# Keys and first values of six gated-DeltaNet heads as seven block products instead of eight

## The chip, the cores and the metric

The kernel runs on one core of one Trainium2 chip. The metric is the device time of one execution in microseconds (us), the median over runs; lower is better. TensorE (PE in the profile) multiplies, VectorE (DVE), ScalarE (ACT) and GpSimd (POOL) do elementwise work, and SyncE (SP) issues nearly all DMAs.

## The reference

Two residual layers over 1024 tokens of width 1024: a gated DeltaNet layer (GDN), then an mLSTM layer, then a final RMSNorm. The change is in the GDN layer, which has 8 heads of 128 key and 256 value columns:

```
p = h @ w_in                                    # h: (1024 tokens, 1024), w_in: (1024, 6160)
qkv, z, a, bt = split(p)
qkv = silu(causal_dwconv(qkv, conv_w))          # 4 taps along the tokens
q = l2norm(q) * 128**-0.5 ;  k = l2norm(k)      # per head
o = gated_delta_chunked(q, k, v, g, beta)       # per head, chunks of tokens, state carried
o = rmsnorm(o, norm_w) * silu(z)
y = o @ w_out
```

Within a head and a chunk, `gated_delta_chunked` forms k k^T with decays, solves a unit lower triangular system, and then walks through the chunks one after the other with a 128 x 256 state.

## The kernel before, in words

**Number format.** Each fp32 operand of a large product is split into two fp32r parts, `hi` (a rounded copy, made on ACT, L261) and `lo` (the rest, made on POOL, or on DVE where an engine is given, L262). A product of two operands is three matmuls: hi*hi, hi*lo, lo*hi. The activations h stand in SBUF transposed, as tiles of 128 features x 512 tokens (two halves of the tokens), split the same way.

**Projection.** A head's 768 columns of `w_in` (128 key, 128 query, 256 value, 256 gate columns z) are computed as three sources of work of two 128-column blocks each: keys with first values (`gkv`), queries with second values (`gqv`), and both gate blocks (`gzp`). The features and the tokens are cut in two, so two column blocks against two token halves are four results, each a sum over two feature halves: eight block products of 4 x 3 = 12 matmuls of 128x512. `Columns` makes the eight products; with `sums=True` it uses A11, S1 = A21 + A22, A12 and A22 of the activations, with the second half's weights as differences. `Pair` makes the same four results from seven products (Strassen's scheme in Winograd's form) with sums S1 to S4 of activation blocks, which stand ready from head 2 on, and with sums of weight blocks, made on DVE; its partial results are then added up on DVE out of PSUM. Before the change, heads 2 to 7 use `Columns(sums=True)` for `gkv` and `Pair` for `gqv` and `gzp`: 32 + 28 + 28 = 88 steps, where a step is three matmuls of 128x512.

**Order of the work.** TensorE's order is written out by hand: the generators of all heads' products run one after the other, and after the n-th step of a head the small generators that stand in `plan` for that step issue their own work. The tables `KEYS`, `QUERIES`, `SOLVE`, `MERGE`, `TOKENS`, `SCAN` (steps after the head's first one; the last entry holds for heads 2 to 7) and `PACE` place them. A number past the head's length falls into the next head. The other engines' orders are set by a scheduler when the program is built. Each engine runs its own list in order; a waiting instruction holds up everything behind it there.

**What a head does besides**, by its functions: `conv_silu` takes a finished result, multiplies and adds the four taps (ACT L291, DVE L298) and applies SiLU (ACT L301). `gdn_keys` transposes the keys (`tpk`), squares them on ACT (`sqrk`), forms `kd`, loads a row of decays (`growb`, DMA), forms the mask `at` = exp(growb + mask - g) with DVE L877 and ACT L880, forms `kk` = k k^T on PE and `nt` on DVE L893, and sends `nt` through DRAM into `nd` (L899, L902). `gdn_solve` runs 31 pairs of small DVE operations on `nd` (`pr`, `xt`, L939 and L941) and sends the result through DRAM into `td`. `gdn_merge` completes the inverse: a DVE product and two transposes give `t`, then four rounds of small matmuls `xp`, `yp`, `xl`, `yl` with copies in between, five steps of the plan, each 4 steps behind the last. `gdn_scan` walks over the 8 chunks: `ks` (PE), `rr` (DVE), `y` (PE), `w` (ACT), `sn` (PE), new state `S` (DVE), `o` (PE), and a transpose `go` for the output gate. `gdn_tokens` transposes the values (`gvp`). The scan, the merge and the tokens of head h run among the products of head h+1.

**Buffers.** PSUM has eight banks, by tags: p 2, b 1, x 1, c 2 (scan), d 2 (all of `tpk`, `kk`, `kq`, `gvp`, `go` and the four merge rounds share these two). In SBUF the tag `rowb` has one buffer of 128x512: `growb` of both halves (and the decay rows of the queries) pass through it, and also the running sum u2 of `gqv`. A buffer is given to the next tile once the last reader of the present one is done, also where that reader comes later in the program.

Of the kernel before, what the change touches and what calls it, by code (L numbers as in the profile page):

```python
# [9 lines left out]
F32 = mybir.dt.float32  # L10
# [3 lines left out]
ALU = mybir.AluOpType  # L14
# [3 lines left out]
P = 128  # L18
# [5 lines left out]
DK = 128  # L24
# [34 lines left out]
TOKENS = ((37, 37, 81, 85), (71, 74, 97, 103), (64, 68, 107, 110))  # L59
# [9 lines left out]
def hybrid_kernel(ctx, tc, x_in, norm_w, final_norm_w, gdn_w_in, gdn_conv_w, gdn_a_log, gdn_dt_bias, gdn_norm_w,  # L69
# [18 lines left out]
    def pwork(name, tag="b"):  # L88
        return pw.tile([P, 512], F32, tag=tag, bufs=banks[tag], name=name)
# [166 lines left out]
    def split(raw, name, tiles=None, e=None, scale=None):  # L256

        shape = list(raw.shape)
        hi, lo = tiles or (wp.tile(shape, F32R, tag=f"ws_{n}", bufs=3, name=f"{name}_{n}") for n in ("hi", "lo"))
        if scale is None:  # L260
            A.copy(hi, raw)  # L261
            (e or G).tensor_tensor(lo, raw, hi.bitcast(F32), ALU.subtract)  # L262
# [209 lines left out]
    def product(ps, block, parts, first=True):  # L472

        hi, lo = parts
        for k, (bhi, blo) in enumerate(blocks[block]):
            if k:
                yield
            for i, (w_, h_) in enumerate(((hi, bhi), (hi, blo), (lo, bhi))):
                mm(ps, w_[:, k, :], h_, start=first and k == 0 and i == 0, stop=k == 3 and i == 2,  # L479
                   skip_group_check=True)  # L480
# [12 lines left out]
    class Columns:  # L493
# [32 lines left out]

        def products(self):
            for e, tags in enumerate(("pp", "bx")):
                ps = [pwork(f"{self.name}_ps{e}{half}", tags[half]) for half in range(2)]
                top = operand()  # L530
                yield from product(ps[0], "A11", top)
                yield
                yield from product(ps[1], "S1" if self.sums else "A21", top)
                yield
                for half in range(2):
                    if half == 0 or self.sums:
                        bottom = operand()
                    yield from product(ps[half], ("A12", "A22")[half], bottom, False)
                    self.sink(e, half, ps[half])
                    yield  # L540

    class Pair:
# [31 lines left out]
        def products(self):  # L574
# [39 lines left out]
            sink(0, 1, c21)  # L614
            yield


    ready, sources = [], []

# [9 lines left out]
    def operand():  # L629
        ahead(LOOK + 1)  # L630
        return ready.pop(0)
# [160 lines left out]
    def gdn_columns(h, st):  # L792

        st["vt"], st["v"] = {}, []

        def dst(e):
            def of(half):
                t = st["vt"][e, half] = hp.tile([P, TH], F32, tag="acc", bufs=3, name=f"gvT{h}_{e}_{half}")
                return t

            return of

        vs = [conv_silu(gcw, 32, 2 * H + 2 * h + e, dst(e), f"gv{h}_{e}") for e in range(ET)]
        v0 = 2 * QK + h * DV
        sinks_of = lambda *sinks: lambda e, half, src: sinks[e](half, src)
        if h == 0:
            return [Columns(gdn_w_in, v0, v0 + P, f"gv{h}", sinks_of(*vs), small=True)]
        k = qk_sink("k", gcw, 32, h, st, "g")
        q = qk_sink("q", gcw, 32, h, st, "g")
        first = Columns(gdn_w_in, QK + h * DK, v0, f"gkv{h}", sinks_of(k, vs[0]), sums=h > 1)  # L810
        if h == 1:
            return [first, Columns(gdn_w_in, h * DK, v0 + P, f"gvq{h}", sinks_of(q, vs[1]))]
# [254 lines left out]
    with tc.manual_schedule(engines={mybir.EngineType.PE}):  # L1067
# [555 lines left out]
```

## Time and profile before

| | |
|---|---|
| median of 3 runs | 1989.7 us (1989.58 to 1993.05) |
| profiled execution: time / span | 1988.66 us / 1986.9 us |
| PE busy | 1900.5 us, 96% of the span |
| DVE busy | 1293.0 us, 65% |
| ACT busy | 1010.6 us, 51% |
| POOL busy | 699.9 us, 35% |
| mean granted TensorE clock | 0.984 |

How to read it: the GDN heads 2 to 7 run from 234.8 to 800.95 us of the span. A busy share of PE of 96% doesn't say that matmuls run at their rate, since the durations of neighbouring matmuls overlap; the distance between their starts does.

### The profile page before, as it was taken

The numbers are of one execution on the slowest core, as the hardware profiler recorded it, in microseconds if no ns is written. First come the engines' busy times: TensorE is split into PE (matmuls) and PEld (weight loads), VectorE is DVE, ScalarE is ACT, GpSimd is POOL, SyncE is SP. The second block draws the span as 40 slices with busy tenths as digits, with TensorE's granted clock in tenths as the row PEclk, the third lists the DMA queues.
The fourth block names the chain that finished last, engine by engine and source line by source line (L and its number), as shares of the span: only waits on it lengthen the run. The fifth ranks groups of instructions, "written<-read, shape, count | busy, mean of one in ns | idle before, by whom it ended". The sixth has DMA issues, their size and how long they took to land.

```text
span 1986.9 us, 28860 instructions
## 1 busy us (share of the span) xinstructions
PE 1900.5 (96%) x9768; PEld 1561.3 (79%) x9768; DVE 1293.0 (65%) x2911; ACT 1010.6 (51%) x2325; POOL 699.9 (35%) x621
## 2 busy tenths in 40 slices
PE   5989999999999999999999899999999999999987
PEld 3777787878787878787878778888888888878876
DVE  7688586858595858548555966666766666673313
ACT  5435454646465555546435555545454555564423
POOL 4243333333333333101021434343333333354553
PEclk9999999999999999999999999999999999999988
DMA  4211122222222222646321122212122222246332
GB/s 139 87 38 51 54 70 70 62 76 58 77 62 67 70 67 77 193 124 219 122 75 55 59 80 65 74 59 75 54 85 64 75 67 65 79 137 204 104 117 75
DMA packets 138620, 171.24 MB, mean 86 GB/s; under 512 B 30860, under 2 KB 68584, under 8 KB 138472
## 3 DMA queue, kind: packets, MB, share of 16 engines
q1 hardware_dynamic: 138472, 169.40, 27.4%
q8 instruction: 77, 1.26, 0.3%
q14 instruction: 71, 0.58, 0.1%
HBM read 142.87 MB, written 26.48 MB: 85 GB/s over the span
## 4 chain that ended last, share of the span: by engine, by line
PE 73%; DVE 14%; DMA 5%; ACT 4%; issue 3%; POOL 1%; SPq 1%; DVEq 0%; ACTq 0%; POOLq 0%
PE lout L678 8%; PE gout L678 7%; PE mv_ps L479 6%; PE gkv_ps L479 6%; PE mkq_ps L479 6%; PE mz_ps L479 6%; PE mog_ps L479 6%; PE gqv_ps L479 5%; PE gzp_ps L479 3%; DMA growb<-g_dram 1%; PE mo L1452 1%; PE mv_ps L1209 1%; DVE gvT L298 1%; PE y L1020 1%; PE out L383 1%
## 5 line engine op out<-in xcount | busy, mean ns | idle before, releaser
L393 POOL TENSOR_TENSOR g_r<-g_r,mhalf 128x1 f32<-128x1 f32 x64 | 41.0, 640 | 220.5 <-DVE g_r L392 203.0
L267 DVE SCALAR_TENSOR_TENSOR gw_lo<-gw_raw,rest,gw_hi 128x256 fp32r<-128x256 f32 x128 | 61.0, 513 | 66.0 <-ACT gw_hi L266 63.4
L262 POOL TENSOR_TENSOR lw_lo<-lw_raw,lw_hi 128x512 fp32r<-128x512 f32 x56 | 72.8, 1302 | 74.9 <-ACT lw_hi L261 71.2
L678 PE MATMUL lout<-lgp_hh,lw_hi 128*128 128x512 f32 x224 | 89.4, 399 | 4.3 <-DVE y L1411 3.2
L262 POOL TENSOR_TENSOR mog_lo<-mog_raw,mog_hi 128x512 fp32r<-128x512 f32 x39 | 50.5, 1294 | 114.5 <-ACT mog_hi L261 114.5
L262 POOL TENSOR_TENSOR mz_lo<-mz_raw,mz_hi 128x512 fp32r<-128x512 f32 x39 | 53.8, 1381 | 98.3 <-ACT mz_hi L261 98.3
L678 PE MATMUL lout<-lgp_hl,lw_hi 128*128 128x512 f32 x224 | 88.4, 395 | 0.0
L678 PE MATMUL lout<-lgp_hh,lw_lo 128*128 128x512 f32 x224 | 87.3, 394 | 0.0
L266 ACT ACTIVATE gw_hi<-gw_raw,rest 128x256 fp32r<-128x256 f32 x128 | 58.1, 502 | 55.2 <-PE gout L678 38.9
L262 POOL TENSOR_TENSOR mv_lo<-mv_raw,mv_hi 128x512 fp32r<-128x512 f32 x38 | 52.0, 1369 | 83.9 <-ACT mv_hi L261 48.0
L479 PE MATMUL gkv_ps<-hh,gkv_hi 128*128 128x512 f32 x176 | 81.3, 462 | 0.0
L262 POOL TENSOR_TENSOR gkv_lo<-gkv_raw,gkv_hi 128x512 fp32r<-128x512 f32 x40 | 52.7, 1317 | 78.2 <-ACT gkv_hi L261 65.9
L262 POOL TENSOR_TENSOR gzp_lo<-gzp_raw,gzp_hi 128x512 fp32r<-128x512 f32 x38 | 49.7, 1309 | 68.0 <-ACT gzp_hi L261 57.0
L261 ACT CAST lw_hi<-lw_raw 128x512 fp32r<-128x512 f32 x56 | 34.8, 621 | 75.2 <-PE lout L678 56.5
L262 POOL TENSOR_TENSOR mkq_lo<-mkq_raw,mkq_hi 128x512 fp32r<-128x512 f32 x35 | 47.1, 1347 | 71.5 <-ACT mkq_hi L261 60.7
L479 PE MATMUL gkv_ps<-hh,gkv_lo 128*128 128x512 f32 x176 | 70.4, 400 | 0.0
L479 PE MATMUL gkv_ps<-hl,gkv_hi 128*128 128x512 f32 x176 | 70.4, 400 | 0.0
L393 POOL TENSOR_TENSOR m_r<-m_r,mhalf 128x1 f32<-128x1 f32 x64 | 44.9, 702 | 71.9 <-DVE m_r L392 70.9
L678 PE MATMUL gout<-glp_hh,gw_hi 128*128 128x512 f32 x160 | 66.7, 417 | 0.0
L678 PE MATMUL gout<-glp_hl,gw_hi 128*128 128x512 f32 x160 | 62.6, 391 | 0.0
L678 PE MATMUL gout<-glp_hh,gw_lo 128*128 128x512 f32 x160 | 62.6, 391 | 0.0
L262 POOL TENSOR_TENSOR gqv_lo<-gqv_raw,gqv_hi 128x512 fp32r<-128x512 f32 x30 | 38.6, 1288 | 65.1 <-PE sn L1027 25.2
(761 smaller groups left out, 6735.6 us busy)
## 6 DMA issues: line engine op xcount, KB each, us to landing
gw_raw<-in_gdn_w_out_dram SPq DMA_DIRECT2D x64, 256.0 KB, 2.6
lw_raw<-in_mlstm_w_out_dram SPq DMA_DIRECT2D x56, 256.0 KB, 2.7
gzp_raw<-in_gdn_w_in_dram SPq DMA_DIRECT2D x32, 256.0 KB, 3.2
growb<-g_dram SPq DMA_DIRECT2D x32, 256.0 KB, 3.1
gg_dram<-gv_h SPq DMA_DIRECT2D x64, 128.0 KB, 1.9
gl<-gg_dram SPq DMA_DIRECT2D x32, 256.0 KB, 3.4
mog_raw<-in_mlstm_w_in_dram SPq DMA_DIRECT2D x32, 256.0 KB, 3.2
mz_raw<-in_mlstm_w_in_dram SPq DMA_DIRECT2D x32, 256.0 KB, 3.0
```

Of the source, the lines that this page charges most:

```text
L261: A.copy(hi, raw)
L262: (e or G).tensor_tensor(lo, raw, hi.bitcast(F32), ALU.subtract)
L266: A.activation(hi[:, k], raw[:, k], AF.Copy, scale=c)
L267: V.scalar_tensor_tensor(lo[:, k], raw[:, k], c, hi.bitcast(F32)[:, k], ALU.mult, ALU.subtract)
L298: V.scalar_tensor_tensor(d_[:, d:], ps[:, :TH - d], col(3 - d), d_[:, d:], ALU.mult, ALU.add)
L383: mm(ps, a[:, e, ds], b[:, e, hs], start=m == 0, stop=m == 3 * ET - 1)
L393: G.tensor_tensor(r, r, mhalf[:, :1], ALU.pow)
L479: mm(ps, w_[:, k, :], h_, start=first and k == 0 and i == 0, stop=k == 3 and i == 2, skip_group_check=True)
L678: mm(pss[2 * j + i], a[:, e, i * P:(i + 1) * P], b, start=h == heads[0] and e == 0 and m == 0, stop=h == heads[-1] and e == ET - 1 and m == 2)
L1020: mm(yp[:, :DV], st["tt"][half][:, cc, :], rr, start=True, stop=True)
L1209: mm(ps[c], h_[k][half][:, c * P:(c + 1) * P], w_[:, k % 2, :], start=k == 0 and i == 0, stop=k == KT - 1 and i == 2)
L1452: mm(op[:, :DV + 2], q[:, s_], S, start=True, stop=False)
```

## The change

The key and first value blocks of heads 2 to 7 become a subclass of `Pair`, `LeftPair`, with another order of the seven products: both token halves of the keys come first (after steps 12 and 20), both halves of the values last (after step 28). Its u2 takes the `rowb` buffer, and the u2 of `gqv` goes to another one. A head is 84 steps instead of 88, and the tables are moved. Core of the diff:

```diff
-KEYS = ((4, 9, 11, 14), (28, 31, 32, 35), (22, 25, 26, 29))
-QUERIES = ((17, 20, 22, 30), (68, 71, 76, 76), (82, 82, 86, 91))
-SOLVE = (27, 44, 32)
-MERGE = ((78, 82), (86, 93), (86, 100))
+KEYS = ((4, 9, 11, 14), (28, 31, 32, 35), (22, 25, 26, 28))
+QUERIES = ((17, 20, 22, 30), (62, 71, 76, 76), (74, 78, 80, 84))
+SOLVE = (27, 44, 38)
+MERGE = ((78, 82), (86, 93), (90, 100))
...
-SCAN = (91, 113, 102)
-PACE = ((3, 3, 8), (4, 3, 10), (4, 3, 11))
+SCAN = (91, 113, 103)
+PACE = ((3, 3, 8), (4, 3, 10), (4, 3, 9))
...
+    class LeftPair(Pair):
+        def operands(self):
...
+            yield part(1, b11, G)
+            V.tensor_tensor(b12, b12, b22, ALU.subtract)
+            V.tensor_tensor(b11, b11, b12, ALU.subtract)
+            yield part(6, b11, e6)
+            yield part(2, b21, G)
+            yield part(7, b12, G)
+            V.tensor_tensor(b21, b21, b11, ALU.subtract)
+            yield part(4, b21, G)
+            V.tensor_tensor(b11, b22, b11, ALU.subtract)
+            yield part(5, b11, e5)
+            yield part(3, b22, G)
+        def products(self):
...
+            yield from product(p1, "A11", operand())
+            A.copy(u2, p1)
...
+            yield from product(p6, "S2", operand())
+            V.tensor_tensor(u2, u2, p6, ALU.add)
...
+            yield from product(p1, "A12", operand(), False)
+            sink(0, 0, p1)
...
+            yield from product(p7, "S3", operand())
+            V.tensor_tensor(u3, u2, p7, ALU.add)
...
+            yield from product(p7, "A22", operand(), False)
+            V.tensor_tensor(p7, u2, p7, ALU.add)
+            sink(0, 1, p7)
...
+            yield from product(p5, "S1", operand())
+            V.tensor_tensor(u3, u3, p5, ALU.add)
...
+            yield from product(p5, "S4", operand(), False)
+            V.tensor_tensor(p5, u2, p5, ALU.add)
+            sink(1, 0, p5)
+            sink(1, 1, u3)
...
-        first = Columns(gdn_w_in, QK + h * DK, v0, f"gkv{h}", sinks_of(k, vs[0]), sums=h > 1)
...
-        return [first, Pair(gdn_w_in, h * DK, v0 + P, f"gqv{h}", sinks_of(q, vs[1]), u2=(hp, "rowb", 1), in_psum=(True, False),
-                            bank="b")]
+        return [LeftPair(gdn_w_in, QK + h * DK, v0, f"gkv{h}", sinks_of(k, vs[0]), u2=(hp, "rowb", 1), bank="b"),
+                Pair(gdn_w_in, h * DK, v0 + P, f"gqv{h}", sinks_of(q, vs[1]), in_psum=(True, False), bank="b")]
...
-            base += (64, 96)[h] if h < 2 else 88
+            base += (64, 96)[h] if h < 2 else 84
```

What the built programs hold: matmul instructions on PE fall by 72 and POOL's instructions by 6, DVE's rise by 54 and ACT's by 22; the number of DMAs stays. Head 5 serves for the places that the prediction speaks of. In the changed program the lines from L612 on stand 53 lines lower: L877, L880, L893, L939, L991 are L930, L933, L946, L992, L1044 there. Names carry the head, the half and a running number, `gkv5_u2` being the running sum of head 5's first pair.

DVE, where head 5's masks `at` are formed. Before:

```order
L877 TENSOR_TENSOR at5_0_5639<-growb05_0_5637,cmask_128 128x512
L877 TENSOR_TENSOR at5_1_5714<-growb05_1_5712,cmask_128 128x512
L991 COPY tt4_1_5466<-yl4_1_5661 64x4x64
L872 TENSOR_TENSOR kd5_5625<-tpk5_0_5626,ekd_285 128x512
L882 TENSOR_SCALAR sk5_5620<-sk5_5620 128x4
L564 TENSOR_TENSOR gqv5_raw0_5258<-gqv5_raw0_5258 128x512
```

And with the change, from the last reader of u2 (L665) on:

```order
L665 TENSOR_TENSOR gkv5_ps5_5582<-gkv5_u2_5375,gkv5_ps5_5582 128x512
L925 TENSOR_TENSOR kd5_5635<-tpk5_1_5716,ekd_285 128x512
L935 TENSOR_SCALAR sk5_5630<-sk5_5630 128x4
L936 RECIPROCAL b5_5631<-sk5_5630 128x4
L295 SCALAR_TENSOR_TENSOR gv5_0_edge_309<-gkv5_ps5_5582,gcw_159,gv5_0_edge_309 128x2
L567 TENSOR_TENSOR gqv5_raw1_5286<-gqv5_raw1_5286,gqv5_raw0_5283 128x512
L937 TENSOR_TENSOR b5_5631<-b5_5631,beta_281 128x4
L295 SCALAR_TENSOR_TENSOR gv5_0_edge_309<-gkv5_ps5_5582,gcw_159,gv5_0_edge_309 128x1
L298 SCALAR_TENSOR_TENSOR gvT5_0_0_5739<-gkv5_ps5_5582,gcw_159,gvT5_0_0_5739 128x511
L1044 COPY tt4_1_5507<-yl4_1_5768 64x4x64
L298 SCALAR_TENSOR_TENSOR gvT5_0_1_5748<-gkv5_u3_5497,gcw_159,gvT5_0_1_5748 128x511
L930 TENSOR_TENSOR at5_0_5649<-growb05_0_5647,cmask_128 128x512
```

The masks moved from ahead of the key transposes' readers to behind the sums of the values, and the copy of `yl4_1` (head 4's last merge round) now stands behind a convolution tap of the values.

PE at the same place, the end of the first pair. Before, `yl4_1` is 23 rows ahead of `kk5_1`; with the change they are neighbours:

```order
L479 MATMUL gkv5_ps5_5582<-S4hh3_2364,gkv5_3_lo_5530 128x512
L479 MATMUL gqv5_ps1_5756<-hh0_0_0_234,gqv5_1_hi_5589 128x512
L479 MATMUL gqv5_ps1_5756<-hl0_0_0_235,gqv5_1_hi_5589 128x512
L479 MATMUL gqv5_ps1_5756<-hh0_0_0_234,gqv5_1_lo_5590 128x512
L1073 MATMUL y4_1_5764<-rr4_1_5670,tt4_0_5411 128x256
L1023 MATMUL yl4_1_5768<-tt4_1_5507,xls4_1_5677 64x64 x4
L943 MATMUL kk5_1_5779<-gkT5_1_5564 128x128 x4
L479 MATMUL gqv5_ps1_5756<-hh0_1_0_240,gqv5_1_hi_5589 128x512
```

`yl4_1` and `kk5_1` use the same one of the two d banks, as the other one holds `kk5_0` until `nt5_0` is formed; between them stands DVE's copy L1044.

ACT, the masks of head 5. Before, from the mask's first half to the second, with no table load between them:

```order
L880 ACT_TABLE_LOAD
L880 ACTIVATE at5_0_5639<-at5_0_5639,gcs_283 128x128 x4
L851 ACTIVATE sqrk5_0_5631,sk5_5620<-tpk5_0_5626 128x128
L261 CAST gqv5_1_hi_5654<-gqv5_raw0_5258 128x512
L851 ACTIVATE sqrk5_0_5631,sk5_5620<-tpk5_0_5626 128x128 x3
L1022 ACTIVATE w4_1_5672<-y4_1_5670,b4_4593 128x256
L880 ACTIVATE at5_1_5714<-at5_1_5714,gcs_283 128x128 x4
```

With the change:

```order
L933 ACT_TABLE_LOAD
L933 ACTIVATE at5_0_5649<-at5_0_5649,gcs_283 128x128 x4
L261 CAST gqv5_5_hi_5829<-gqv5_raw0_5283 128x512
L301 ACT_TABLE_LOAD
L301 ACTIVATE gvT5_0_0_5739<-gvT5_0_0_5739 128x512
L581 COPY gqv5_u2_5755<-gqv5_ps1_5756 128x512
L933 ACT_TABLE_LOAD
L933 ACTIVATE at5_1_5729<-at5_1_5729,gcs_283 128x128 x4
L391 ACTIVATE g4_1_sq_5816,g4_1_r_5815<-o4_1_5812 128x256
L301 ACT_TABLE_LOAD
L301 ACTIVATE gvT5_0_1_5748<-gvT5_0_1_5748 128x512
```

A SiLU of the values now stands between the two exponentials. This is so in heads 3 to 7, two table loads more in each.

SP, the same stretch. Before:

```order
L489 DMA gzp5_raw0_5648<-in_gdn_w_in_dram 128x512 x2
L857 DMA growb05_1_5712<-g_dram_287 128x512
L899 DMA nt_dram5_0_5689<-nt5_0_5684 32x4x32 x4
L902 DMA nd5_5624<-nt_dram5_0_5689 16x1024 x4
L1003 DMA gg_dram_288<-gv4_h0_5149 128x2x128
L899 DMA nt_dram5_1_5777<-nt5_1_5772 32x4x32 x4
L902 DMA nd5_5624<-nt_dram5_1_5777 16x1024 x4
L489 DMA gzp5_raw1_5651<-in_gdn_w_in_dram 128x512 x2
```

With the change:

```order
L910 DMA growb05_0_5647<-g_dram_287 128x512
L910 DMA growb05_1_5727<-g_dram_287 128x512
L952 DMA nt_dram5_0_5704<-nt5_0_5699 32x4x32 x4
L910 DMA growb15_0_6307<-g_dram_287 128x512
L955 DMA nd5_5634<-nt_dram5_0_5704 16x1024 x4
L952 DMA nt_dram5_1_5789<-nt5_1_5784 32x4x32 x4
L489 DMA gzp5_raw1_5586<-in_gdn_w_in_dram 128x512 x2
L955 DMA nd5_5634<-nt_dram5_1_5789 16x1024 x4
```

The last weights of head 5's gates (`gzp5_raw1`) now stand ahead of the second half of `nd`, and wait for a buffer that POOL still reads. The first decay row moved down to the second one; before, it stood six rows further up.

More of the change, by code (lines that the diff above doesn't have):

```diff
@@ L615, in products @@
             yield
+    class LeftPair(Pair):
+        def operands(self):
+            (b11, b12), (b21, b22) = ((raw[:, 0], raw[:, 1]) for raw in self.raws)
+            part = lambda n, raw, e: split(raw, f"{self.name}_{n}", e=e)
+            e6, e5 = self.engines
+            yield part(1, b11, G)
[10 more added lines that the diff above has]
+        def products(self):
+            name, sink = self.name, self.sink
+            pool, tag, bufs = self.u2
+            u2 = pool.tile([P, TH], F32, tag=tag, bufs=bufs, name=f"{name}_u2")
+            p1 = pwork(f"{name}_ps1", "p")
+            yield from product(p1, "A11", operand())
+            A.copy(u2, p1)
+            yield
+            p6 = pwork(f"{name}_ps6", "b")
+            yield from product(p6, "S2", operand())
+            V.tensor_tensor(u2, u2, p6, ALU.add)
+            yield
+            yield from product(p1, "A12", operand(), False)
+            sink(0, 0, p1)
+            yield
+            u3 = wp.tile([P, TH], F32, tag="wraw", bufs=WB, name=f"{name}_u3")
+            p7 = pwork(f"{name}_ps7", self.bank)
+            yield from product(p7, "S3", operand())
+            V.tensor_tensor(u3, u2, p7, ALU.add)
+            yield
+            yield from product(p7, "A22", operand(), False)
+            V.tensor_tensor(p7, u2, p7, ALU.add)
+            sink(0, 1, p7)
+            yield
+            p5 = pwork(f"{name}_ps5", "p")
+            yield from product(p5, "S1", operand())
+            V.tensor_tensor(u3, u3, p5, ALU.add)
+            yield
+            yield from product(p5, "S4", operand(), False)
+            V.tensor_tensor(p5, u2, p5, ALU.add)
+            sink(1, 0, p5)
+            sink(1, 1, u3)
+            yield
     ready, sources = [], []
```

5 lines of the change are left out of this document (3 added, 2 removed).

## The prediction

> **What bounds the kernel now.** I read the page's engine shares first, then TensorE's timeline inside head 5, then the stretches and waits of heads 2 to 7, and last the timelines of DVE, ACT and SP around the place that the change moves.
>
> ```profile
> span 1986.9 us, 28860 instructions
> PE 1900.5 (96%) x9768; PEld 1561.3 (79%) x9768; DVE 1293.0 (65%) x2911; ACT 1010.6 (51%) x2325; POOL 699.9 (35%) x621
> L479 PE MATMUL gkv_ps<-hh,gkv_lo 128*128 128x512 f32 x176 | 70.4, 400 | 0.0
> ```
> ```profile
> 560.43 0.39 PE L479 MATMUL gqv_ps<-S2hl,gqv_hi 128*128 128x512 f32 x1
> 560.66 0.40 PE L479 MATMUL gqv_ps<-S2hh,gqv_lo 128*128 128x512 f32 x1
> 560.90 0.40 PE L479 MATMUL gqv_ps<-S2hh,gqv_hi 128*128 128x512 f32 x1
> 562.29 0.59 PE L1027 MATMUL sn<-w,kd 128*128 128x256 f32 x2
> 562.72 0.59 PE L1036 MATMUL o<-S,gqT 128*128 128x256 f32 x2
> ```
>
> TensorE is busy throughout, but a matmul of 128x512, listed with 0.40 us, follows its forerunner after 0.23 us (560.43, 560.66, 560.90). What a removed matmul is worth is 0.23, not 0.40; a scan product takes 0.43 (562.29 to 562.72).
>
> ```profile
> 517.22:555.89 38.67, 38.29 (x262) 30.20 (x261) 20.99 (x55) 21.50 (x65) 13.58 (x12) 0.98 0.19 56
> 555.89:580.89 25.00, 25.00 (x114) 20.66 (x113) 22.68 (x72) 13.68 (x27) 7.56 (x7) 1.00 0.27 80
> 580.89:611.59 30.70, 29.14 (x160) 24.18 (x158) 23.51 (x64) 15.51 (x39) 14.17 (x11) 1.00 0.25 73
> sum 566.15, PE 551.05 PEld 447.81 DVE 404.70 ACT 308.03 POOL 208.63; mean PE 91.84 PEld 74.64 DVE 67.45 ACT 51.34 POOL 34.77
> ```
> ```profile
> PE xp L970 <- DVE t L961: 11.9, 6, 2.5
> PE kk L890 <- DVE tt L991: 2.1, 5, 0.5
> PE tpk L848 <- DVE kd L872: 1.1, 1, 1.1
> ```
>
> The first three rows are head 5's keys with first values, queries with second values, and gates: 38.67 + 25.00 + 30.70 = 94.37 us. The sum row holds the six heads, 94.4 us each. DVE works 22.68 of 25.00 us in the middle stretch and TensorE doesn't wait there. The waits are TensorE's in those 566 us: about 2 us a head where the merge begins (xp), 0.4 at kk, and little else.
>
> ```profile
> 609.78 0.44 PE L970 MATMUL xp<-t,nt 32*32 32x32 f32 x16 [1.56 <-DVE t L961]
> ```
> ```profile
> 324.30:327.50 3.20, 3.20 (x10) 2.53 (x9) 1.73 (x4) 2.28 (x10) 1.10 (x1) 0.50 0.03 8
> 610.00:613.40 3.40, 3.40 (x30) 2.87 (x25) 1.89 (x5) 2.62 (x11) 1.23 (x2) 1.00 0.13 39
> 798.80:802.00 3.20, 3.20 (x10) 2.63 (x9) 1.44 (x4) 3.09 (x13) 0.00 (x0) 0.50 0.36 124
> ```
>
> Behind the xp waits of heads 2, 3, 4 and 7 the granted clock is 0.50 for some 3.4 us (first and last of four shown), behind those of heads 5 and 6, the two shortest, 1.00 (610.00). A half clock costs half of it, 1.7 us. The Trainium skill ("TensorE: Matmul & The Clock Gate", the table on why it matters) asks for no idle gap over about 3 us; here gaps below that already halve the clock, so the rows decide.
>
> **The change, part by part.** My sum is against the profiled execution, 1988.66 us (1.0 below the median), and goes head by head.
>
> *TensorE's work.* 12 matmuls fewer in each of six heads: 72 x 0.23 = -16.6 us. All of it lies on TensorE's own path.
>
> *Added work beside it.* Per head DVE gets 9 operations of 128x512, at about 0.6 from start to start 5.5 us; ACT one cast and one copy, POOL one subtraction less. DVE's mean goes from 67.45 to 73 us in a head of 94: it fits as a sum, so I price only what is late for somebody. The DMAs are as many as before.
>
> *The masks.* u2 of the first pair holds `rowb` until L665, so the first `growb` can't start before the first pair ends. The rows that price this chain:
>
> ```profile
> 542.90 0.68 DVE L877 TENSOR_TENSOR at<-growb,cmask 128x512 f32<-128x512 f32 x1
> 546.64 0.69 DVE L877 TENSOR_TENSOR at<-growb,cmask 128x512 f32<-128x512 f32 x1 [3.06 <-DMA growb<-g_dram]
> 547.25 0.41 DVE L991 COPY tt<-yl 64x256 f32<-64x256 f32 x1
> 548.67 0.69 DVE L872 TENSOR_TENSOR kd<-tpk,ekd 128x512 f32<-128x512 f32 x1 [1.01 <-ACT sqrk L851]
> 553.57 0.74 DVE L298 SCALAR_TENSOR_TENSOR gvT<-gkv_ps,gcw,gvT 128x511 f32<-128x511 f32 x1
> 556.40 1.13 DVE L893 SCALAR_TENSOR_TENSOR nt<-kk,nb,at 128x128 f32<-128x128 f32 x4
> 564.22 0.19 DVE L939 TENSOR_TENSOR pr<-xt,nd 128x31 f32<-128x31 f32 x1 [0.66 <-DMA nd<-nt_dram]
> 581.09 0.69 DVE L613 TENSOR_TENSOR gqv_u<-gqv_u,gqv_ps 128x512 f32<-128x512 f32 x1 [0.16 <-PE gqv_ps L479]
> 599.40 0.17 DVE L941 TENSOR_TENSOR xt<-xt,pr 128x8 f32<-128x8 f32 x1
> 607.74 0.69 DVE L958 TENSOR_TENSOR tt<-td,dmask 128x512 f32<-128x512 f32 x1 [1.42 <-DMA td<-tb_dram]
> 609.20 0.43 DVE L961 STREAM_TRANSPOSE t<-tt 64x256 f32<-64x256 f32 x1
> ```
> ```profile
> 544.24 1.28 ACT L880 ACT_TABLE_LOAD   x1
> 545.53 1.28 ACT L880 ACTIVATE at<-at,gcs 128x128 f32<-128x128 f32 x4
> 548.27 0.28 ACT L851 ACTIVATE sqrk<-tpk 128x128 bf16<-128x128 f32 x1
> 551.61 0.69 ACT L291 ACTIVATE gvT<-gkv_ps,gcw 128x512 f32<-128x512 f32 x1
> 557.08 1.28 ACT L301 ACT_TABLE_LOAD   x1
> ```
> ```profile
> 543.61 0.33 SPq L857 DMA_DIRECT2D growb<-g_dram  x1
> 560.52 1.70 SPq L902 DMA_DIRECT2D nd<-nt_dram  x4
> 562.95 1.28 POOL L262 TENSOR_TENSOR gqv_lo<-gqv_raw,gqv_hi 128x512 fp32r<-128x512 f32 x1 [5.04 <-PE sn L1027]
> ```
>
> I walk it for heads 3 to 7 in the new order, with t = 0 where the first pair's last matmul has been issued; these are estimates from the rows above.
>
> - L665 runs from 0.2 to 0.9 (581.09). ACT finishes four squares of `tpk5_1` (0.4 each) and the value tap (0.69) by 2.2. DVE needs kd 0.69, then behind ACT an edge, L567 0.68, an edge, a tap 0.74, and only then the copy of `yl4_1` (0.41): t = 4.4. `kk5_1` uses that bank; TensorE would be there at 1.4 (three matmuls, y, yl). Wait: 3.0, against 0.4 now.
> - The first `growb` is issued at 0.9 and lands 3.0 later (543.61 to 546.64), so DVE is what sets its mask: 5.7, its exponentials 7.0. Then ACT's list holds a cast 0.6, a SiLU table load 1.28 that waits for the values' third tap (9.1), SiLU 0.6, a copy 0.6, the load back 1.28, four exponentials 1.28: 14.1. `nt5_1` is complete at 14.5. DVE's `rr4_2` stands behind it; TensorE waits at `go4_0` (bank of `kk5_0`, free at 9.5) and at `y4_2` (15.0), together 2.0.
> - `nd5_1` now stands behind `gzp5_raw1` on SP, which waits for POOL's `lo` of a weight cast at 16.9 (1.28 more: 18.2). Two DMA issues later, 19.1, and 3.7 from issue to use (560.52 to 564.22): the solve begins at 22.8. `rr4_3` is behind that, and `w4_2` was late behind the loads: another 0.9 of waiting. All waits so far: 3.0 + 2.0 + 0.9 = 5.9.
> - The solve took 35.3 us (564.22 to 599.57), with DVE full. In its new stretch stand two more block additions, a state update and a residual, one tap fewer: 36.6, end at 59.4. To `td` 8.2 (599.57 to 607.74): 67.6. To t, 1.9 now; a second tt, an `at` product and a weight difference stand ahead of it: 3.1, so xp is ready at 70.7.
> - TensorE's way to xp took 52.3 us (555.89 to 608.2, where its wait begins). With merges 4 steps later and heads 4 shorter there are 24 matmuls more in between, 5.5, and some 14 scan, key and transpose products, 5.9: 63.7, with the waits 69.6. So xp still waits, 1.1.
> - In the first pair `gvp4_1_1` now needs the bank of `tpk5_0`, that is, kd, behind four squares: 1.0.
>
> Sum of waits in each of five heads: 5.9 + 1.1 + 1.0 = 8.0, together 40.0. In head 2 no merge ends there and ACT has two loads, not four; 3.0, between 0 and the others' 8.0, nearer to its own few waits now. What goes: xp 11.9, kk and tpk 3.2, half clock 4 x 1.7 = 6.8. I set no half clock after: a wait of 1.1 is shorter than those that left the clock full, and after the 3.0 of kk a slow TensorE only spends what it would wait at `go4_0` and `y4_2` anyway. 1988.66 - 16.6 - 21.9 + 43.0 = 1993.2, rounded to **1993**. Ends of the doubtful terms: the walk's 8.0 can be 4 (if the solve starts on time) or 11.
>
> The two extra loads cost 1.28 us each by the rows: the exponentials at 545.53 follow the load at 544.24 at once. The Trainium skill ("ScalarE: Activation LUTs", on what ACT_TABLE_LOAD costs) states about 1283 ns for the load and 1380 ns more to drain, 2.66 in all; no drain shows here. By that figure, an estimate, the two switches ahead of the second exponentials would put the solve 2.8 later and the sum near 2007.
>
> **PACE.** A state update now has 2 steps instead of 4 before the next `ks`. Two steps and two o products give 1.4 + 0.9; S takes 0.47 in DVE's list. I set 0; late by 0.3 a chunk it would be 2 a head.
>
> **The rivals.**
> *Faster: the late solve is hidden.* If DVE, no longer interrupted, ends the solve as TensorE's step 79 passes, xp never waits, and the waits behind kk are half of mine: 3.0 + 1.4 + 1.0 = 5.4 in five heads, 3.0 in head 2: -16.6 - 21.9 + 30 = -8.5, **1980**. For it: DVE full at 22.68 of 25.00 held nobody up. Against it: in-order lists; `rr4_2` and `rr4_3` stand behind the masks.
> *Faster: only the matmuls count*, waits and clock as they are: -16.6, **1972**. Against it: u2 holds `rowb` to the end.
> *Slower: DVE paces the heads.* If solve and masks end 3 us later than I have it, every head 3 to 7 is 3 longer and the xp wait of 4 halves the clock again, 1.7: 5 x 4.7 = 23, **2017**; it decides from 2 us on. Against it: 73 of 94 us as a sum.
>
> **How the numbers follow.** A measurement of this kernel tells about 0.2%, 4 us, from no change. My forecast, that nearly all is given back, 1984 to 2004: 0.45 (0.05 of it faster, 0.18 same, 0.22 slower). Hidden solve 0.24, matmuls alone 0.13: faster. DVE pacing 0.18: slower. So faster 0.42, same 0.18, slower 0.40. The range 1968 to 2010 takes in both faster cases and leaves the far end of the slower one out.
>
> **What would show it.** Right: 72 matmuls of L479 fewer; the first pair near 34 us; a new TensorE wait of 2 to 4 us at kk (L943) for DVE L1044 in five heads; two table loads at L933 in each of heads 3 to 7, one in head 2; the first `pr` some 20 us and more after the first pair's end, now 8.3; heads of 92 to 97 us. Wrong: heads of 90 or less, no wait at kk, `pr` within 15 us; or waits at ks and rr in the queries' stretch, which I have at nothing.

## The result, and the profile after

The changed kernel takes 2010.39 us (median of 4 runs, 2008.44 to 2013.62), the kernel before 1989.84: ratio 1.0103, interval 1.0084 to 1.0121. The profiled execution took 2010.67 us. The change makes the kernel 1.0% slower; the forecast was 1993 (1968 to 2010).

First the page's shares:

```profile
span 2009.0 us, 28772 instructions
PE 1894.1 (94%) x9696; PEld 1546.2 (77%) x9696; DVE 1333.4 (66%) x2965; ACT 1027.1 (51%) x2347; POOL 689.6 (34%) x615
```

Then the stretches of head 5 (keys with first values, queries with second values, gates) and, in one row, heads 2 to 7. Columns as before: length, then busy time of PE, PEld, DVE, ACT, POOL, the granted clock, the DMA share, GB/s.

```profile
530.89:565.31 34.42, 31.45 (x238) 23.93 (x236) 20.94 (x44) 15.73 (x43) 12.00 (x10) 1.00 0.17 50
565.31:601.32 36.01, 30.93 (x140) 24.43 (x138) 26.22 (x78) 21.66 (x49) 9.09 (x10) 0.95 0.29 81
601.32:630.80 29.48, 29.48 (x146) 24.53 (x145) 26.70 (x78) 16.99 (x48) 12.38 (x10) 1.00 0.20 64
234.83:825.14 590.31, 547.10 (x3029) 435.63 (x3028) 437.33 (x1176) 323.82 (x819) 201.88 (x173) 0.98 0.22 66
```

The 72 matmuls are gone (9768 to 9696). The first pair of head 5 is 4.3 us shorter (38.67 to 34.42) and the gates 1.2 (30.70 to 29.48), but the middle stretch, which had no wait, is 11.0 longer (25.00 to 36.01). Not all of that is lost time: some of TensorE's work moved there from its neighbours (the middle row counts 140 matmuls instead of 114), and of the 36.01 us TensorE idled 5.1. Heads 2 to 7 take 590.31 us instead of 566.15, 24.2 more; the rest of the program is 2.1 us shorter. TensorE stands idle for 590.31 - 547.10 = 43.2 us there, before for 15.1. Its waits in these heads, in all, how often, the longest:

```profile
PE y L1073 <- DVE rr L1070: 10.5, 10, 2.2
PE kk L943 <- DVE tt L1044: 7.5, 5, 1.5
PE gkv_ps L479 <- DVE gkv_u L654: 5.4, 6, 1.2
PE yl L1023 <- DVE kd L925: 5.0, 5, 1.0
PE gkv_ps L479 <- DVE gkv_u L662: 4.5, 6, 0.8
PE go_gp L355 <- DVE nt L946: 2.7, 2, 2.2
PE xp L1023 <- DVE t L1014: 2.1, 3, 1.0
PE y L1073 <- DVE pr L992: 1.7, 1, 1.7
PE go_gp L355 <- ACT gv_h L1093: 1.5, 4, 0.6
PE kk L943 <- DVE kd L925: 1.2, 1, 1.2
PE sn L1080 <- ACT w L1075: 1.1, 1, 1.1
```

The wait at xp has gone from 11.9 to 2.1. Ten others are listed now, of which only the one at kk for L1044 was there before, with 2.1. In head 5, in TensorE's timeline:

```profile
548.71 0.50 PE L479 MATMUL gkv_ps<-hh,gkv_hi 128*128 128x512 f32 x1 [0.78 <-DVE gkv_u L654]
559.43 0.49 PE L479 MATMUL gkv_ps<-S4hh,gkv_hi 128*128 128x512 f32 x1 [0.78 <-DVE gkv_u L662]
567.60 0.67 PE L1023 MATMUL yl<-tt,xls 64*64 64x64 f32 x8 [1.00 <-DVE kd L925]
569.77 1.34 PE L943 MATMUL kk<-gkT 128*128 128x128 f32 x8 [1.50 <-DVE tt L1044]
581.02 0.70 PE L1073 MATMUL y<-rr,tt 128*128 128x256 f32 x2 [0.33 <-DVE rr L1070]
592.22 0.67 PE L1073 MATMUL y<-rr,tt 128*128 128x256 f32 x2 [2.24 <-DVE rr L1070]
```

The first two are joints inside the new pair: S3 and A22 go into one PSUM bank, and so do S1 and S4, and between them DVE has to read the bank (L654, L662). The next two are the bank of `yl4_1`, which waits for kd, and that of `kk5_1`, which waits for the copy of yl. The last two are the scan, behind the late masks and the late solve. In DVE's timeline of the same stretch (the first pair ends at 565.31):

```profile
565.51 0.70 DVE L665 TENSOR_TENSOR gkv_ps<-gkv_u,gkv_ps 128x512 f32<-128x512 f32 x1 [3.10 <-PE gkv_ps L479]
569.31 0.40 DVE L1044 COPY tt<-yl 64x256 f32<-64x256 f32 x1
570.30 0.68 DVE L930 TENSOR_TENSOR at<-growb,cmask 128x512 f32<-128x512 f32 x1
579.18 1.23 DVE L946 SCALAR_TENSOR_TENSOR nt<-kk,nb,at 128x128 f32<-128x128 f32 x4 [1.86 <-ACT at L933]
588.96 0.69 DVE L563 TENSOR_TENSOR gzp_raw<-gzp_raw,gzp_raw 128x512 f32<-128x512 f32 x1 [3.88 <-DMA gzp_raw<-in_gdn_w_in_dram]
590.75 0.18 DVE L992 TENSOR_TENSOR pr<-xt,nd 128x31 f32<-128x31 f32 x1
```

ACT's cast ahead of the second mask, that mask with its table load, and SP's queue:

```profile
574.39 0.62 ACT L261 CAST gqv_hi<-gqv_raw 128x512 fp32r<-128x512 f32 x1 [2.10 <-PE gqv_ps L479]
577.45 1.28 ACT L933 ACT_TABLE_LOAD   x1
578.74 1.28 ACT L933 ACTIVATE at<-at,gcs 128x128 f32<-128x128 f32 x4
```
```profile
584.23 0.83 SPq L489 DMA_DIRECT2D gzp_raw<-in_gdn_w_in_dram  x2
585.23 1.72 SPq L955 DMA_DIRECT2D nd<-nt_dram  x4
```

The first mask comes 5.0 us behind the end of the pair, where it came 13.0 ahead of it (542.90 against 555.89), and the solve begins 25.4 behind it instead of 8.3. The last stretch of that was not in the forecast: DVE stands 3.88 us at L563 for the gate weights, whose DMA had to wait on SP, and the solve and `rr` stand behind it in DVE's list.

### The profile page after: what moved, and what is told of

It reads as the page before. It is cut to its first block, busy times and chain, and to the rows that moved or that the text cites. A ratio compares the mean times of both kernels' runs of the same rounds, so it can differ in the third digit from the quotient of the medians.

```text
span 2009.0 us, 28772 instructions
## 1 busy us (share of the span) xinstructions
PE 1894.1 (94%) x9696; PEld 1546.2 (77%) x9696; DVE 1333.4 (66%) x2965; ACT 1027.1 (51%) x2347; POOL 689.6 (34%) x615
## 4 chain that ended last, share of the span: by engine, by line
PE 63%; DVE 20%; ACT 5%; DMA 5%; issue 3%; POOL 2%; SPq 2%; DVEq 0%; ACTq 0%; POOLq 0%
PE gout L731 8%; PE lout L731 7%; PE mv_ps L479 6%; PE mz_ps L479 6%; PE mkq_ps L479 6%; PE mog_ps L479 6%; PE gkv_ps L479 5%; DVE gvT L298 2%; PE gqv_ps L479 2%; DVE pr L992 2%; PE gzp_ps L479 1%; PE mo L1505 1%; PE mv_ps L1262 1%; DVE gqT L298 1%; DVE xt L994 1%
## 5 line engine op out<-in xcount | busy, mean ns | idle before, releaser
L262 POOL TENSOR_TENSOR gkv_lo<-gkv_raw,gkv_hi 128x512 fp32r<-128x512 f32 x34 | 45.6, 1341 | 92.6 <-ACT gkv_hi L261 77.6
L391 ACT ACTIVATE g_sq<-o 128x256 bf16<-128x256 f32 x64 | 24.4, 381 | 81.3 <-PE o L1090 81.1
L1093 ACT ACTIVATE gv_h<-o,g_r 128x256 f32<-128x256 f32 x64 | 30.2, 471 | 59.1 <-POOL g_r L393 59.0
L479 PE MATMUL gzp_ps<-hh,gzp_hi 128*128 128x512 f32 x136 | 59.0, 434 | 0.0
L1513 ACT ACTIVATE mo_g<-mo,m_r 128x256 f32<-128x256 f32 x64 | 30.4, 474 | 54.9 <-POOL m_r L393 54.9
```

Of the source, the lines that this page charges most:

```text
L391: A.activation(junk, o_ps[:, :DV], AF.Square, accum_out=r)
L1093: A.activation(v, op[:, :DV], AF.Copy, scale=r)
L1513: A.activation(g, op[:, :DV], AF.Copy, scale=r)
```

## The experiments

All times are medians, the ratios those to the kernel before on the same chip. "Heads" is the length of heads 2 to 7 in the profiled execution (before 566.2, changed 590.3). Each experiment builds on the changed kernel unless it says otherwise.

**The wait at kk, moved away.**

```diff
-KEYS = (..., (22, 25, 26, 28))
+KEYS = (..., (22, 25, 30, 33))
```

> The changed kernel with one table entry moved: KEYS of heads 2 to 7 from (22, 25, 26, 28) to (22, 25, 30, 33), so that the second half's tpk and kk stand 4 and 5 steps later. Theory W (the loss is TensorE's own waits, each with its price, and the half clock behind them): the waits at yl (5.0 us) and at kk (7.5 + 1.2) and the tail of some 0.17 us at each of 11 go, 15.6 us, and with them the four half-clock windows that begin within 3.4 us of kk (heads 4 to 7, 1.7 each, 6.8): 2010.4 - 22 = 1988, up to 1998 if the masks of the second half, now later, add up to 2 us a head to the waits at y. Rival D (DVE paces the heads, TensorE's waits only show where it is caught): the waits move to y and xp, the time stays within 4 us of 2010.

2013.01 us, 1.0115 (1.009 to 1.014); heads 592.6. No gain. The waits at kk and yl are gone, and of TensorE's waits now these are new or larger:

```profile
PE go_gp L355 <- DVE kd L925: 10.9, 5, 2.2
PE sn L1080 <- ACT w L1075: 9.1, 6, 1.7
PE xp L1023 <- DVE t L1014: 7.3, 4, 2.9
```

The bank that kd releases late now makes `go` wait instead of `yl`. TensorE's idle time in heads 2 to 7 rose in all (43.2 to 48.8 us), and the time at half clock fell (23.9 to 13.7). Taking away the waits at kk and yl, 13.7 us together, gained nothing by itself: here the rival was right.

**The joints, taken apart.** S1 between S3 and A22, on top of the step above; the weight parts 4 and 5 change places with it, and the keys' second half is ready 4 steps later.

```diff
             yield from product(p7, "S3", operand())
             V.tensor_tensor(u3, u2, p7, ALU.add)
             yield
-            yield from product(p7, "A22", operand(), False)
-            V.tensor_tensor(p7, u2, p7, ALU.add)
-            sink(0, 1, p7)
-            yield
             p5 = pwork(f"{name}_ps5", "p")
             yield from product(p5, "S1", operand())
             V.tensor_tensor(u3, u3, p5, ALU.add)
             yield
+            yield from product(p7, "A22", operand(), False)
+            V.tensor_tensor(p7, u2, p7, ALU.add)
+            sink(0, 1, p7)
+            yield
```

> As e1_kk_later, and LeftPair takes S1 between S3 and A22, so that no product goes on into a PSUM bank right behind the DVE sum that reads it; the second half of the keys is ready 4 steps later. Theory W: the waits at L654 (5.4 us) and L662 (4.5) and twelve tails of 0.17 go: 12 us less than e1_kk_later, 1974 to 1986. Rival D: no wait of TensorE is worth its length; within 4 us of e1_kk_later. Theory K (the keys' second half ready 4 steps later makes everything behind it late): a new wait at tpk or kk, slower than e1_kk_later.

1996.92 us, 1.0043 (1.003 to 1.0055); heads 578.0, 14.6 less than the step before, where the two waits and their tails made 12. Both waits are gone. The agreement of the two sizes is a net, though: the wait of sn for w fell too (9.1 to 1.1 us) and y's for rr (6.2 to 1.2), those of xp and go rose (7.3 to 11.6 and 10.9 to 13.1), and the time at half clock rose from 13.7 to 30.7. So the joints' part of the 14.6 is not shown to be 12.

**The masks without `rowb`.** The decay row goes by DMA straight into the tile of the mask.

```diff
-            grow_b = decay_row(0, h, half)
             st["at"][half] = at = hp.tile(...)
+            nc.sync.dma_start(at.rearrange("p c t -> p (c t)"), g_dram[0, h, ...].partition_broadcast(P))
             ...
-                V.tensor_tensor(at, grow_b.rearrange(...), cmask..., ALU.add)
+                V.tensor_tensor(at, at, cmask..., ALU.add)
```

> The changed kernel with the decay row of the masks loaded straight into the tile of the mask (at) instead of into rowb; nothing else. The prediction's theory R (u2 holds rowb to the end of the first pair, so the masks and the solve are late): masks some 4 us earlier in each head, the first pr within 20 us of the first pair's end instead of 25, the waits at y (10.5 + 1.7 us) and at go for nt (2.7) gone, and the half-clock windows behind them in heads 2, 3 and 4 (1.7 each): -15 to -20, 1990 to 1996. Rival L (DVE stands before the solve at L563 for the gate weights, whose load waits for a weight buffer, whatever the masks do): the solve begins as late as before, 2006 to 2010.

1996.18 us, 1.0039 (1.0025 to 1.0054); heads 576.9, and head 2 begins 4.8 us earlier (the profiled execution, 1992.14, is the fastest of ten). The first pair of head 5 ends at 553.74 there, and

```profile
568.47 0.19 DVE L992 TENSOR_TENSOR pr<-xt,nd 128x31 f32<-128x31 f32 x1 [3.01 <-DMA nd<-nt_dram]
```

so the solve begins 14.7 us behind it instead of 25.4: the theory that u2 in `rowb` makes the masks late holds, and the theory that the gate weights hold the solve up whatever the masks do does not. But a new wait of TensorE stands at `gvp`, for ACT's copy of xl (L1041), 13.0 us in five heads, with the half clock behind four of them.

> e2_apart and e3_row_in_at together. If theories W and R hold, the gains add: 1960 to 1976, below the kernel before (1989.8). If L holds instead of R, as e2_apart within 4 us. If D holds, near 2005.

2002.65 us, 1.007 (1.005 to 1.009); heads 583.1. The two gains, 16 and 14, don't add: together they are worse than either, with xp at 13.0, gvp at 10.8 and kk at 7.7 us of waiting.

**Each next wait by itself.** Four kernels: e6 and e7 take one thing away each on top of the row in `at`, e8 joins both, and e9 puts the row in `at` into the kernel before:

```diff
-TOKENS = (..., (60, 64, 103, 109))     # e6, on top of the row in at
+TOKENS = (..., (60, 64, 103, 116))
```

> e3_row_in_at with one table entry moved: the last gvp of heads 2 to 7 at step 116 instead of 109, so that it no longer stands among the merge's last rounds and kk for the same two PSUM banks. Theory B (the two d banks are the limit: gvp waits 13.0 us for the copy of xl there, and the clock is half behind it in four heads): -13.0 -0.9 (five tails) -6.8 (four half windows) = -21, some 1975. Rival D (DVE paces the heads, whatever wait is taken away): the wait turns up at kk, yl, xp or y, within 5 us of e3_row_in_at (1996).

1994.47 us, 1.0036 (1.0022 to 1.0049). The same 13.0 us now stand at kk, for the same copy on ACT:

```profile
PE kk L943 <- ACT xls L1041: 13.0, 5, 2.6
```

Moving gvp moved the wait, and its releaser stayed the copy; e11 below moves the copy itself.

> e3_row_in_at with S3 taken before A12 (its result in the bank of tag p, that of S1 in tag b), so that the first of the two joints, where a product goes on into the bank that DVE has just to read, is gone and the keys' halves are ready at steps 16 and 20. Theory J (a joint costs its wait and a tail wherever it stands): -5.4 - 1.0 = -6.4, about 1990. Rival D: within 2 us of e3_row_in_at.

2010.88 us, 1.0106 (1.0083 to 1.0129). The first joint is gone, but the result of S1 and S4 now lies in the one bank of tag b until the taps of the values have read it, and the next pair's p6 waits for that:

```profile
PE gqv_ps L479 <- DVE gvT L298: 16.8, 6, 6.7
```

> e6_row_tokens and e7_row_order together, and tpk of the first half at step 23 instead of 22, so that it stands in the second joint. Theories B and J: -21 - 6.4 - 4 = -31 from e3_row_in_at, about 1965, well below the kernel before. Rival D: not below 1985.

2008.72 us, 1.0093 (1.0066 to 1.012): the same loss at the same bank (13.4 us).

> The kernel before with the decay row of the masks loaded straight into at; nothing else. In the changed kernel this took 4.8 us out of heads 0 and 1 and the rest out of heads 2 to 7. Theory R (the row's buffer was a limit only since u2 of the first pair lies in it): heads 2 to 7 as before, heads 0 and 1 up to 5 us shorter: 1984 to 1989. Rival G (the row held up the kernel before too, where DVE stood 3.06 us for growb in each head): 1970 to 1980.

1987.19 us, 0.9991 (0.9975 to 1.0007): no difference that can be told. In the kernel before, the row in `rowb` cost nothing, though DVE stood 3.06 us for it in a head.

**ACT's list.** On top of e6, e10 forms both halves' masks behind one another, one pair of table loads a head instead of two; e11 moves one copy besides.

```diff
-            A.copy(xs[64:], xp[64:])
+            (V.tensor_copy if half else A.copy)(xs[64:], xp[64:])
```

> e6_row_tokens with both halves' masks formed behind one another once the keys' first half is done: one pair of ACT table loads a head instead of two. In e6_row_tokens kk waits 13.0 us for ACT's copy xls, which stands behind a mask, a table load and a SiLU. Theory A (ACT's list, with the table loads that the change put between the masks, is what the wait at xl is made of, not the PSUM banks): two loads and a mask less ahead of the copy, 2.6 to 3.8 us, so the 13.0 go, and the two half windows; 1994 - 13 - 1 - 3 = 1977. Rival B (the two d banks are simply too few there): the wait stays within 3 us of its size, time within 5 us of e6_row_tokens. Rival D (DVE paces): the wait goes to kd, nt or t, time within 5 us.

2006.33 us, 1.0098 (1.0077 to 1.0118), 12 slower than e6. Fewer table loads did not help: the copy now stands behind both masks, kk waits 16.0 instead of 13.0, and the second joint grew from 5.7 to 9.3. Other waits shrank, so that TensorE's idle time grew by 2.7 us in all. The half clock took more: four of its five stretches now last 6.83 us, and the time at half is 30.7 us instead of 6.8. TensorE worked 24.0 and 6.8 us in it; at half speed half of that is lost, an estimated 8.6 us more. Both together are 11.3, where heads 2 to 7 are 10.0 longer. The rows of these heads, e6 and then e10, the length first and then PE's busy time:

```profile
231.34:808.71 577.37, 540.63 (x3030) 429.93 (x3028) 444.24 (x1176) 330.80 (x822) 200.27 (x173) 0.99 0.23 66
232.93:820.26 587.33, 547.95 (x3030) 436.88 (x3028) 444.07 (x1176) 314.81 (x810) 200.14 (x173) 0.97 0.22 65
```
```profile
PE kk L947 <- ACT xls L1045: 16.0, 5, 3.2
PE gkv_ps L479 <- DVE gkv_u L662: 9.3, 6, 1.6
```

> e10_masks_together with the copy of xl of the second half on DVE instead of ACT (it is the third quarter of the merge's last rounds; that of yl is on DVE already). Theory A: within 3 us of e10 if e10 took the wait away, or the wait goes now if a square or a cast still held the copy up. Rival D: slower by up to 10 us, as DVE gets 0.4 us more a head at its fullest place.

1988.79 us, 0.9995 (0.9983 to 1.0008), 17.5 less, and no half-clock window at all in heads 2 to 7:

```profile
231.46:803.36 571.90, 538.45 (x3030) 426.77 (x3028) 448.38 (x1182) 312.27 (x804) 199.35 (x173) 1.00 0.23 67
```
```profile
PE kk L947 <- DVE xls L1045: 3.2, 5, 0.6
```

So it was the copy's place in ACT's list. Of the 15.4 us by which heads 2 to 7 got shorter (587.33 to 571.90), TensorE's idle time gives 5.9; the larger part is the half clock, which went from 30.7 us to none. The same edit in the changed kernel, where masks and keys are late anyway:

> The changed kernel with only the copy of xl of the merge's second half on DVE instead of ACT. Of the step from e10 to e11, 17.5 us, this tells whether it is the copy alone. There kk waited for that copy; in the changed kernel it waits for the copy of yl behind it. Theory A (ACT's list): up to 5 us faster than 2010. Theory R (rowb, the late masks, first): 2007 to 2012, since kk waits for kd and for yl's copy on DVE, which then has 0.4 us more ahead of it.

2011.86 us, 1.0118 (1.009 to 1.0146): nothing.

**Keys, solve and merge against each other.** From e11 on, the joints apart (e12), then tpk and kk of the second half later (e13), then the merges and the scan later (e14).

```diff
-KEYS = (..., (22, 25, 26, 28))          # e12: (22, 25, 30, 33)
+KEYS = (..., (22, 25, 34, 37))          # e13, e14
-TOKENS = (..., (60, 64, 103, 116))
+TOKENS = (..., (60, 64, 103, 122))
-MERGE = (..., (90, 100))
+MERGE = (..., (96, 106))                # e14 only
-SCAN = (91, 113, 103)
+SCAN = (91, 113, 109)                   # e14 only
```

> e11_xls_on_dve with the joints taken apart (S1 between S3 and A22, keys' second half at steps 30 and 33 as in e2_apart) and the last gvp at step 122. If joints cost what the profile shows (5.4 + 5.7 us and twelve tails, 13 us) and nothing later gives it back: 13 us less than e11, near 1965. In e5_apart_row the same step, on top of the row in at, cost 6 us instead: if the later second half of the keys is the reason (kk and nt 5 steps later, the solve at 24 instead of 15 us behind the first pair), it is again slower than e11, by 5 to 10 us, with the wait at xp back.

1994.17 us, 1.0027 (1.0012 to 1.0041), 5 slower than e11, with 20.5 us at half clock where e11 has none. The joints' 14.7 us of waiting are gone; tpk waits 19.4 for the SiLU of the keys' second half on ACT, and the solve begins 27.2 us behind the first pair (575.35 against 548.19).

> e12_apart_masks with the second half of the keys later, KEYS (22, 25, 34, 37). There tpk waited 19.4 us in all for ACT's SiLU of the keys, with a half-clock window behind it in five heads. Theory W (each wait is worth its length where nothing stands behind it): the second half of nt comes no later than now, so 19.4 + 1 + 8.5 go and xp, 6.1 now, takes back what the solve is then late, at most 4 us in each of five heads: 1994 - 29 + 0 to 20 = 1965 to 1985. Rival D (the chain from the keys through masks, solve and merge to the scan sets the period of a head, whatever TensorE waits for): the wait moves to xp in full, 1990 to 1996.

1995.99 us, 1.0041 (1.0027 to 1.0055). tpk's 19.4 are gone and come back elsewhere:

```profile
PE xp L1027 <- DVE t L1018: 12.7, 6, 6.0
PE ks L1072 <- DVE S L1089: 10.7, 9, 1.7
```
```profile
574.99 0.19 DVE L996 TENSOR_TENSOR pr<-xt,nd 128x31 f32<-128x31 f32 x1 [2.44 <-DMA nd<-nt_dram]
```

The first pair ends at 546.33 there: the solve begins 28.7 us behind it.

> e13_tpk_later with the merges 6 and 10 steps later, MERGE (96, 106), and the scan 6 steps later (109). If in e13 xp waits for the late solve, this takes up to 4 us a head of it: 10 to 20 us below e13. If a head's period is set by a chain that runs through the scan (buffers of at and tt come free with the last chunks), it is slower than e13, with new waits at kk, nt or the masks.

1978.26 us, 0.9943 (0.9923 to 0.9963): 11 us below the kernel before and 32 below the changed one. Its heads take 557.2 us.

```profile
561.53 0.19 DVE L996 TENSOR_TENSOR pr<-xt,nd 128x31 f32<-128x31 f32 x1 [1.67 <-DMA nd<-nt_dram]
```
```profile
PE xp L1027 <- ACT gv_h L891: 8.7, 5, 1.8
PE kk L947 <- DVE kd L925: 5.3, 5, 1.1
PE gvp L890 <- DVE gv_h L358: 4.3, 4, 1.2
```

The first pair ends at 538.93: the solve begins 22.6 behind it, 6 earlier than in e13, though the keys' places were not touched. What moved away from them is the merge of the head before, 6 steps for both entries, and with it the start of its scan. TensorE's idle time fell from 33.1 to 22.1 us and the half clock rose from none to 13.7; the heads are 13.4 us shorter, so some 9 us of the gain stand in neither count and stay open.

> e11_xls_on_dve with the first tpk at step 23 instead of 22, so that it stands between S1 and S4, in the second joint, where TensorE waits 9.3 us in six heads. Theory J (a joint costs what no other work fills): tpk with 0.6 us fills a part, -3 to -5 us, 1984 to 1986. Rival D: within 1 us of e11.

1992.22 us, 1.0021 (1.0008 to 1.0033), 3 slower than e11 by the medians, with intervals that just meet: the joint's wait fell by 1.1 us, the wait of tpk for kd rose by 4.7 (3.4 to 8.1) and y's for rr by 2.6 (2.1 to 4.7).

> e14_merge_later with three table entries moved for the two d banks: the third gvp from step 103 to 92 and the last from 122 to 126, the second kk from 37 to 38. There xp waits 8.7 us for ACT's copy of a gvp (L891), kk 5.3 for kd, gvp 4.3 for the gate product (L358), and three half-clock windows stand behind the first. Theory W: these waits and windows go, 18 + 5 us, less what DVE then holds up: 1960 to 1970. Rival D: within 4 us of 1978.

1986.35 us, 0.9987 (0.9976 to 0.9998), 8 slower than e14. The waits at xp and kk went; that of gvp for L358 grew from 4.3 to 10.7, and two new ones came (go for a copy of the merge 7.3, tpk for another 5.8), with 20.5 us at half clock instead of 13.7.

> The kernel before with its merges 4 steps later, MERGE (90, 104), and the scan one step later (103). It tells whether e14's gain is that of the later merges alone. If the kernel before was held by xp (11.9 us of waits and four half-clock windows, 6.8), it gains 12 to 19 us, 1971 to 1978, and seven products have brought nothing. If its merges were placed where the solve allowed it, and the waits go to y and ks behind them, it stays within 4 us of 1989.

1987.03 us, 0.9991 (0.9977 to 1.0004); heads 566.2, as before. xp no longer waits, and kk waits 8.2 us for the copy of xl and 4.4 for kd. So merges 4 steps later and a scan 1 step later gain nothing that can be told in the kernel before; e14's own step, 6 and 6, was not tried there. e14 was not tried with eight products, so how much of its 11 us the seven bring is not separated from its other edits.

## Why the prediction was wrong, point by point

- **The matmuls**, -16.6: 72 fewer, as said. Nothing in the runs speaks against 0.23 each.
- **kk and its bank**, 3.0 a head: 1.00 at yl and 1.50 at kk, with two tails 2.8. Right in size, and by the mechanism named (kd, the copy L1044, one bank): the copy ends at 4.4 behind the pair (569.31 + 0.40), as forecast. That yl would share the wait was not seen, so kk alone shows 1.5, below the 2 to 4 given as its sign.
- **The masks**, the first at 5.7 behind the pair, the exponentials done at 14.1, nt at 14.5: 5.0, 14.7 (578.74 + 1.28) and 15.1 (579.18 + 1.23). Right, and the row in `at` shows the cause. The table load costs 1.28 us as set: the exponentials at 578.74 follow the load at 577.45 at once.
- **The solve**, from 22.8: it began at 25.4. The walk had `gzp_raw1` ahead of `nd` on SP, but not L563, which waits for the same DMA on DVE. `rr` is behind it: the term of 0.9 for `rr4_3` is a wait of 2.24 in head 5, and y's waits for rr and pr are 12.2 us in all.
- **xp**, 1.1 in five heads, 5.5: 2.1. **gvp**, 1.0 in five: none. Too high by 8.4 together. **PACE**, set at 0: no wait at ks is listed.
- **The joints** are missing. That product A22 goes on in the bank of S3 right behind its sum, and S4 in that of S1, stands in the change's listing, and I costed only DVE's time for these sums, not TensorE's wait for them: 5.4 + 4.5 us, and twelve tails. With the tails that is 11.9 us, put at nothing. The experiment that takes them apart gives 14.6 in the heads, net of other waits and of the clock.
- **The half clock**, "I set no half clock after": there are seven windows of 3.4 us at half, 11.9 us. Three stand behind what the late masks and solve hold up (go for nt in head 2, y for rr in heads 3 and 4) and four behind kk (heads 4 to 7). The step that failed is that a slow TensorE spends only what it would wait for afterwards. In head 5 the window (570.61 to 574.02) was full of matmuls at half speed, and the chain that y waits for stood behind the same matmuls: ACT's cast ahead of the second mask waited 2.10 us for them (574.39). So that chain was held up too, and the wait at y behind it is 0.33; the 2.24 at the next y comes 16 us behind the window's end. No run takes the half clock away by itself, so that all of the 11.9 is loss is argued from these rows and not shown.
- **The tail of a wait.** A matmul is listed with 0.40 and followed after 0.23, so a wait by the profile starts 0.17 late. With 44 waits listed now and 12 before that is 5.4 us, which the sum had not.

The measured terms give -16.6 - 21.9 (what goes) + 43.2 (idle now) + 11.9 (half clock) + 5.4 = 22.0 us for heads 2 to 7, which are 24.2 longer: 2.2 us of them stay open. The rest of the program is 2.1 shorter. Only because these two cancel does 1988.66 + 22.0 = 2010.7 meet the profiled 2010.67; that is chance. That my waits, 43.0, agree with the 43.2 is chance too: 9.9 of these are the joints, and xp and gvp have 8.4 less. So three steps of the sum failed: TensorE's wait at the joints, the half clock and the tails were put at nothing. The heads, forecast at 92 to 97 us, take 94.3 to 101.4, and the range ended 0.4 us below the result.

Of the rivals, "DVE paces the heads" put the time at 2017 by a later solve and the half clock at xp. Its size was nearest; its place was not, since xp hardly waits. A sharper form of it is what the experiments support: a head's period isn't the sum of TensorE's waits. Taking the wait at kk away (e1), that at gvp (e6) or at tpk (e13) gained at most 2 us, as other waits came in its place. My reading, which no single run proves, is that the keys of one head and the merge and scan of the head before meet in the same few steps, in two PSUM banks and in the lists of ACT and DVE. The change made that meeting closer: with heads 4 steps shorter and MERGE's second entry left at 100, the last merge round went from step 24 of the next head to step 28, onto kk, which had moved from 29 to 28. Gains came from what is ahead of that place (masks, joints, the copy on ACT) and from parting the two (e14). That e14's solve begins 6 us earlier with the same KEYS is the row that speaks for it; it isn't proof that only this moved.

## What to carry to other kernels

Cost a reordered accumulation by its joints: a product that goes on in a bank which another engine has just to read pays that read on TensorE (here 0.8 to 1.2 us at a joint), unless another product stands between. Follow a moved buffer's release through each in-order list to the next reader, and look for every instruction that waits for the same DMA. And where one wait has been taken away for nothing, compare who holds the resource: here three table entries that keep two heads' small work apart (17.7 us from e13 to e14) were worth more than the wait at xp that they were moved for (12.7). Count the time at half clock beside the waits: from e10 to e11 it was the larger part of the gain.

## What the runs showed of the hardware

The half clock does not follow the longest gap. In these profiles it comes in windows of 3.41 us, sometimes two in a row, and mostly follows a window in which TensorE worked for less than about 45%. Two pairs of windows of the kernel before, behind xp at the end of head 2 and at the end of head 5, and then one pair of the changed kernel, behind kk in head 5:

```profile
320.79:324.20 3.41, 1.31 (x22) 0.86 (x21) 3.25 (x7) 0.84 (x2) 0.07 (x1) 1.00 0.19 70
324.20:327.61 3.41, 3.41 (x11) 2.74 (x10) 1.94 (x4) 2.37 (x11) 1.21 (x1) 0.50 0.03 7
607.51:610.92 3.41, 1.85 (x26) 1.33 (x25) 2.40 (x6) 0.27 (x1) 1.25 (x1) 1.00 0.40 109
610.92:614.33 3.41, 3.41 (x39) 2.56 (x37) 2.38 (x5) 2.35 (x11) 1.30 (x1) 1.00 0.00 0
```
```profile
567.20:570.61 3.41, 1.51 (x15) 1.38 (x16) 3.38 (x11) 2.61 (x5) 1.36 (x2) 1.00 0.24 81
570.61:574.02 3.41, 3.41 (x11) 2.73 (x11) 3.41 (x9) 1.28 (x4) 0.00 (x0) 0.50 0.23 77
```

PE worked 1.31 and 1.51 of 3.41 us (38 and 44%) ahead of the half clock, 1.85 (54%) ahead of the full one. In the changed kernel no single wait there was over 1.5 us: yl's and kk's together were enough. In the 19 profiles of this study, by the clock's records and TensorE's rows, 86 stretches at half clock begin in heads 2 to 7. Before 66 of them TensorE had worked less than 45% of the 3.41 us, before the other 20 between 45 and 65%; of 3115 windows at full speed, 4 stand behind one under 45%. So the share tells most cases and is no sharp limit, and what decides the others is open. If this holds, where a wait falls against these windows decides on up to 1.7 us, which would explain why waits of the same length cost differently from head to head; no run moves a wait against the windows by itself.
